# The output projection's and the MLP's lo parts on GpSimd: one operation of 1024 columns, or two of 512

## The chip, the cores and the metric

The kernel runs on one core of one Trainium2 chip. The metric is the device time of one execution in microseconds, the median over several runs. The engines are named as the profile names them: PE is TensorE (PEld its weight loads), DVE is VectorE, ACT is ScalarE, POOL is GpSimd, and SPq is the queue of SyncE, from which this kernel issues all of its DMAs.

## The reference, cut to what matters

Two layers of an encoder on a sequence of 1024 tokens, model width 1024, all in float32:

```python
h = rms_norm(x) * (1.0 + sc1) + sh1
z = h @ w_in[l]                       # three groups of heads: attention A, attention B, recurrence C
x = x + g1 * (jnp.concatenate([o_a, o_b, o_c], axis=-1) @ w_out[l])
h = rms_norm(x) * (1.0 + sc2) + sh2
x = x + g2 * (jnp.square(jax.nn.relu(h @ w_ff1[l])) @ w_ff2[l])     # 1024 -> 4096 -> 1024
```

## The kernel before, in words

Every product is made of three matmuls (`mm3`, lines 291 to 294): an operand is split into a rounded high part `hi` and a remainder `lo`, and hi by hi, hi by lo and lo by hi are added up in PSUM.

The weights come in **units** of 128 partitions by 1024 columns (`wunit`, lines 279 to 289). For each unit the SP queue issues one DMA of 512 KB into `w_raw` (line 284), ACT casts it into `w_hi` (line 286), and one subtraction makes `w_lo` (line 288). While the input projection runs, the subtraction is on DVE; from the end of the recurrence C on (`early_weights`), for the output projection and the whole MLP of that layer, it is on POOL: 224 of the 272 units.

From there on two pools are in use in turn (`wp = [f_["w"], w_first]`, rotated by `wunit`), each with one buffer for `w_raw` and two each for `w_hi` and `w_lo`. So a unit's DMA has to wait until the unit before it in the same pool has its `w_lo` (its raw buffer is free then), and a unit's cast has to wait until PE is done with the unit two places before it in the same pool.

The tokens are worked on in two halves of 512. The first half's output projection and a part of its MLP run while the second half's attention is still at work; then comes the second half's output projection, then groups of MLP weights used for both halves (`ffn_both`), and then the **last loop** of a layer: `ffn_half` of the second half alone over 8 groups. In `ffn_half` a group has four units: **a** and **b**, the two units of `w_ff1`, and **c** and **d**, the two units of `w_ff2`. They alternate between the pools: a and c are in one, b and d in the other. The code asks for the next group's a and b ahead of this group's c and d, so the order in one pool is c of the group before, next a, c, the a after it, and so on. PE uses each of these units for 24 matmuls with 512 columns. A product with a and b goes into a PSUM tile `mm`, then relu (ACT, 1119), square (ACT, 1120, and DVE, 1121) and a difference (POOL, 1122) make `act`; a product with c and d goes into PSUM tiles `S`, which DVE adds to x (1144).

The order of the instructions on each engine and in each queue isn't that of the text: the program is built with a scheduler that has a timing model of its own (`schedule_with_timeline_sim=True`) and puts each instruction where that model finds room. What stands in a queue is then worked off in that order.

Of the kernel before, what the change touches and what calls it, by code (L numbers as in the profile page):

```python
# [10 lines left out]
F32 = mybir.dt.float32  # L11
# [9 lines left out]
D = 1024  # L21
# [136 lines left out]
def tile_hybrid_encoder(ctx: ExitStack, tc: tile.TileContext, I, out, depth=DEPTH, dbg=None):  # L158
# [5 lines left out]
    def hp(k):  # L164
        return tc.high_priority(offset=HP[k]) if k in HP else nullcontext()
# [71 lines left out]
    def modulation_sums():  # L237

        while mod_pending:
            l, pc_, acc = mod_pending.pop(0)  # L240
            with hp("mod"):
                ps = (mmt, auxt)[MODAUX]()
                for j in range(4):
                    nc.tensor.matmul(ps[:, j:j + 1], acc[:, j * P:(j + 1) * P], ones[:, 0:1], start=True, stop=True)
            m = modc[l][:, pc_ * 4:pc_ * 4 + 4]
            nc.vector.tensor_add(m, m, ps[:, 0:4])
            if pc_ // 2 in (1, 4):
                nc.vector.tensor_scalar_add(m, m, 1.0)
# [26 lines left out]

    raw_bufs = [2]
    lo_eng = [nc.vector]

    def wunit(pool, src):
        if isinstance(pool, list):  # L280
            pool.append(pool.pop(0))
            pool = pool[-1]
        raw = pool.tile([P, D], F32, name="w_raw", tag="w_raw", bufs=raw_bufs[0])
        dma(raw, src)
        hi = pool.tile([P, D], F32R, name="w_hi", tag="w_hi")
        nc.scalar.copy(hi, raw)  # L286
        lo = pool.tile([P, D], F32R, name="w_lo", tag="w_lo")
        lo_eng[0].tensor_sub(lo, raw, hi.bitcast(F32))  # L288
        return hi, lo

    def mm3(ps, wh, wl, ah, al, first, last):
# [567 lines left out]
    def open_pools(specs):  # L859
        c = ExitStack()  # L860
        return c, {n: c.enter_context(tc.tile_pool(name=nm, bufs=b, side=sd)) for n, nm, b, sd in specs}
# [18 lines left out]
    def hook(j):  # L880
        if j == WAT:
            ready.extend(wunit(first_in[1]["w"], I["w_feat"][0, t]) for t in (T_BK, T_BQ))

    with hp("start"):
# [9 lines left out]
        for j in modulation_start(0, q0["m"], hook):  # L894
            b, c = modc[0][:, j:j + 1], modc[0][:, 8 + j:9 + j]
# [7 lines left out]
    for l in range(depth):  # L903
# [8 lines left out]
        wp, tp = w_["w"], w_["tp"]  # L912
        raw_bufs[0] = RAWA
        lo_eng[0] = nc.vector
        pp = const

        pc = pp.tile([P, 4], F32, name=f"pc{l}")
# [49 lines left out]
        def feat_tiles_(jobs):  # L967
            ws = [ready.pop(0) if ready else wunit(wp, I["w_feat"][l, j[0]]) for j in jobs]
            for half in range(2):
                for w, j in zip(ws, jobs):  # L970
                    ps = proj_feat(hT[half], w)
                    with hp('post'):
                        j[1](ps, half)

        def tok_group_(g, post):
            units = [wunit(wp, I["w_tok"][l, g, i]) for i in range(2)]
            for tt in range(0, NCH, 2):
                ps = proj_tok(hT, units, tt)
                with hp('post'):
                    post(ps, tt)  # L980
# [60 lines left out]
        def attend(tok):  # L1041
            k, pr, hq = tok[0], int(tok[1]), int(tok[2])
            with hp("att"):
                if k == "A":
                    attention_a(ap, l, (2 * pr, 2 * pr + 1), hq)
                else:
                    ap["ag"] = None
                    attention_b(ap, l, lamc, subg, (2 * pr, 2 * pr + 1), hq)

        def load_o(half, pool, rows, oT=None):  # L1050
            if oT is None:
                oT = [pool.tile([P, KT, HALF], F32R, name="oT", tag="h") for _ in range(2)]
            for j in rows:
                for i in range(2):
                    dma(oT[i].bitcast(F32)[:, j, :], s.o[j][i, :, half * HALF:(half + 1) * HALF])
            return oT

        for tok in ORDER.split():
            if tok == "C":
                modulation_sums()  # L1060
                wctx.close()
                hctx.close()
                octx, o_ = open_pools([("h", f"o{l}", 2, A)])
                heads0 = load_o(0, o_["h"], OPRE)
                bctx, b_ = open_pools([("c", f"cb{l}", 2, B)])
                cctx, c_ = open_pools([("c", f"ca{l}", 2, A)])

                def early_weights():
                    cctx.close()
                    raw_bufs[0] = 1  # L1070
                    lo_eng[0] = nc.gpsimd
                    wctx, w_ = open_pools([("w", f"w0_{l}", WFB // 2, A)])
                    return wctx, w_["w"], [wunit(w_["w"], I["w_out"][l, j]) for j in range(NEARLY)]

                early = []
                with hp("C"):
                    scan_c(c_["c"], b_["c"], l, pc[:, 3:4], lambda: early.append(early_weights()))
                bctx.close()
            elif tok[0] in "AB":
                attend(tok)  # L1080
            else:
                jobs[tok]()
# [207 lines left out]
```

## Time and profile before

| what | before |
|---|---|
| median of 3 runs | 3304.26 us (3304.03 to 3312.45) |
| the profiled execution, its own time | 3303.55 us |
| its span, first to last instruction | 3301.8 us |
| outside the span | 1.75 us |
| PE busy | 3150.7 us, 95% |
| mean granted clock of PE | 0.971 |
| POOL busy | 1304.7 us, 40%, of which 545.2 us is line 288 |

The time is the profiled execution's; the span is what its trace covers. Busy times of PE are modelled at their ends, so that a stretch in which PE waits for nothing shows 100%.

### The profile page before, as it was taken

How to read it: one execution, taken by the hardware profiler on the slowest of the kernel's cores; microseconds unless marked ns; L12 is line 12 of the kernel's file. 1: busy time of each engine (PE TensorE's matmuls, PEld its weight loads, DVE VectorE, ACT ScalarE, POOL GpSimd, SP SyncE). 2: the span in 40 equal slices, each digit the busy share in tenths (PEclk: the TensorE clock that was granted, in tenths of full speed). 3: DMA queues.
4: the chain of work that ended last, by engine and by line, in shares of the span. 5: the costliest groups of instructions: out<-in, count | busy, mean ns of one | idle time of the engine just before them, and what ended most of it. 6: DMA issues, size and time to landing. Idle time of an engine off the chain costs nothing.

```text
span 3301.8 us, 44789 instructions
## 1 busy us (share of the span) xinstructions
PE 3150.7 (95%) x16604; PEld 2541.8 (77%) x16604; DVE 1949.1 (59%) x2649; ACT 1478.6 (45%) x2847; POOL 1304.7 (40%) x867
## 2 busy tenths in 40 slices
PE   8999989999899999999999999899999999999998
PEld 4887767777678888887878966777777778888786
DVE  6577865557764565546463776555668545333545
ACT  4356656566652311213333666555677422222332
POOL 3343412334455433324534543123345443333453
PEclk8999979999999999999999999899999999999999
DMA  6665374435324244413234633734343421111222
GB/s 246 192 200 189 118 215 135 123 86 168 108 90 169 77 137 134 135 59 102 96 113 127 199 125 124 215 101 141 105 146 94 160 96 52 51 52 51 84 95 77
DMA packets 214458, 411.80 MB, mean 125 GB/s; under 512 B 35928, under 2 KB 92376, under 8 KB 213216
## 3 DMA queue, kind: packets, MB, share of 16 engines
q1 hardware_dynamic: 214240, 408.93, 39.2%
q8 instruction: 132, 2.16, 0.3%
q14 instruction: 86, 0.70, 0.1%
HBM read 335.43 MB, written 73.40 MB: 124 GB/s over the span
## 4 chain that ended last, share of the span: by engine, by line
PE 58%; DVE 6%; DMA 3%; ACT 2%; issue 2%; POOL 2%; SPq 0%; DVEq 0%; ACTq 0%; POOLq 0%
PE mm L292 10%; PE mm L293 10%; PE mm L294 10%; PE S L292 5%; PE S L293 5%; PE S L294 5%; PE aux L482 3%; PE S L450 2%; PE aux L474 2%; PE mm L780 1%; PE mm L403 1%; PE mm L745 1%; PE mm L402 1%; PE mm L404 1%; DVE col L456 1%
## 5 line engine op out<-in xcount | busy, mean ns | idle before, releaser
L288 POOL TENSOR_TENSOR w_lo<-w_raw,w_hi 128x1024 fp32r<-128x1024 f32 x224 | 545.2, 2443 | 490.6 <-ACT w_hi L286 475.3
L292 PE MATMUL mm<-h_hi,w_hi 128*128 128x512 f32 x1472 | 591.1, 403 | 7.9 <-ACT z L436 4.5
L293 PE MATMUL mm<-h_lo,w_hi 128*128 128x512 f32 x1472 | 584.1, 397 | 5.0 <-POOL h_lo L900 3.1
L294 PE MATMUL mm<-h_hi,w_lo 128*128 128x512 f32 x1472 | 580.4, 395 | 0.1
L286 ACT CAST w_hi<-w_raw 128x1024 fp32r<-128x1024 f32 x272 | 281.5, 1049 | 609.0 <-PE S L293 234.2
L456 DVE TENSOR_REDUCE col<-S 128x1 f32<-128x1024 f32 x288 | 350.1, 1224 | 116.9 <-PE S L450 115.6
L1144 DVE SCALAR_TENSOR_TENSOR x<-S,modc,x 128x512 f32<-128x512 f32 (+1 forms) x416 | 283.4, 724 | 228.3 <-PE S L294 228.1
L1121 DVE TENSOR_TENSOR ff_r<-ff_r 128x512 f32<-128x512 f32 x128 | 190.5, 1490 | 318.3 <-ACT act L1120 318.2
L458 ACT ACTIVATE pr<-S,col 128x1024 f32<-128x1024 f32 x288 | 323.8, 1125 | 120.9 <-DVE col L456 60.7
L292 PEld LDWEIGHTS mm<-h_hi,w_hi 128*128 128x128 f32 x1472 | 279.5, 190 | 78.5 <-ACT z L436 5.8
L293 PEld LDWEIGHTS mm<-h_lo,w_hi 128*128 128x128 f32 x1472 | 279.9, 190 | 73.1 <-POOL h_lo L900 5.1
L294 PEld LDWEIGHTS mm<-h_hi,w_lo 128*128 128x128 f32 x1472 | 279.9, 190 | 63.5 <-DVE w_lo L288 0.8
L1122 POOL TENSOR_TENSOR act<-ff_r,act 128x512 fp32r<-128x512 f32 x128 | 169.2, 1322 | 397.6 <-DVE ff_r L1121 394.5
L292 PE MATMUL S<-act,w_hi 128*128 128x512 f32 (+1 forms) x832 | 318.7, 384 | 3.4 <-DVE x L1144 3.2
L293 PE MATMUL S<-act,w_hi 128*128 128x512 f32 (+1 forms) x832 | 317.5, 382 | 1.5 <-POOL act L1122 1.5
L294 PE MATMUL S<-act,w_lo 128*128 128x512 f32 (+1 forms) x832 | 315.0, 382 | 0.8 <-POOL w_lo L288 0.8
L450 PE MATMUL S<-ks,qs 128*128 128x512 f32 x768 | 247.7, 430 | 36.2 <-ACT pr L458 18.9
L1119 ACT ACTIVATE ff_r<-mm 128x512 f32<-128x512 f32 x128 | 76.2, 595 | 409.6 <-PE mm L294 405.6
L474 PE MATMUL aux<-cst,pr 128*128 128x128 f32 x1536 | 234.2, 287 | 19.4 <-DVE pr L590 8.5
L474 PEld LDWEIGHTS aux<-cst,pr 128*128 128x128 f32 x1536 | 188.4, 147 | 67.3 <-issue 18.2
L482 PE MATMUL aux<-pt,vt 128*64 128x256 f32 x1536 | 195.8, 387 | 3.7 <-ACT pt L475 3.7
L475 ACT COPY pt<-aux 128x512 f32<-128x512 f32 x288 | 166.3, 592 | 69.7 <-PE aux L474 68.5
(233 smaller groups left out, 5908.7 us busy)
## 6 DMA issues: line engine op xcount, KB each, us to landing
w_raw<-in_w_ff SPq DMA_DIRECT2D x192, 512.0 KB, 3.3
mw<-in_w_mod SPq DMA_DIRECT2D x160, 256.0 KB, 2.9
ks<-bk SPq DMA_DIRECT2D x192, 128.0 KB, 3.2
lf<-g_st SPq DMA_DIRECT2D x64, 256.0 KB, 3.2
oT<-o SPq DMA_DIRECT2D x64, 256.0 KB, 5.3
lf<-lf SPq DMA_DIRECT2D x16, 1024.0 KB, 5.1
w_raw<-in_w_out SPq DMA_DIRECT2D x32, 512.0 KB, 3.4
w_raw<-in_w_feat SPq DMA_DIRECT2D x28, 512.0 KB, 3.8
```

Source lines behind the costliest of these rows:

```text
L286: nc.scalar.copy(hi, raw)
L288: lo_eng[0].tensor_sub(lo, raw, hi.bitcast(F32))
L292: nc.tensor.matmul(ps, wh, ah, start=first, stop=False)
L293: nc.tensor.matmul(ps, wh, al, start=False, stop=False)
L294: nc.tensor.matmul(ps, wl, ah, start=False, stop=last)
L450: nc.tensor.matmul(sp[:, hh * HALF:(hh + 1) * HALF], q[:, sl], ks[:, hh * HALF:(hh + 1) * HALF], start=i == 0, stop=i == len(qs) - 1)
L456: nc.vector.tensor_reduce(nm, sp, axis=AX.X, op=ALU.max, negate=True)
L458: nc.scalar.activation(p, sp, AF.Exp, bias=nm, accum_out=z)
L474: nc.tensor.transpose(tp[:, j * P:(j + 1) * P], p[:, kt * P:(kt + 1) * P], ident)
L482: nc.tensor.matmul(ps[64 * c:64 * c + 64, 0:256], vt[:, kt, :], pts[c][kt // 4][:, kt % 4, :], start=kt == 0, stop=kt == KT - 1)
L1121: nc.vector.tensor_mul(r, r, r)
L1144: nc.vector.scalar_tensor_tensor(x, sp[:, k * HALF:k * HALF + n], g2[:, j - 1 + k:j + k], x, op0=ALU.mult, op1=ALU.add)
```

## The change

From `early_weights` on, POOL makes each `w_lo` in two subtractions of 512 columns. On DVE it stays one.

```diff
--- before.py
+++ after.py
@@ -275,6 +275,7 @@
     raw_bufs = [2]
     lo_eng = [nc.vector]
+    lo_parts = [1]
@@ -285,7 +286,9 @@
         lo = pool.tile([P, D], F32R, name="w_lo", tag="w_lo")
-        lo_eng[0].tensor_sub(lo, raw, hi.bitcast(F32))
+        n = D // lo_parts[0]
+        for c in range(0, D, n):
+            lo_eng[0].tensor_sub(lo[:, c:c + n], raw[:, c:c + n], hi.bitcast(F32)[:, c:c + n])
         return hi, lo
@@ -912,6 +915,7 @@
         lo_eng[0] = nc.vector
+        lo_parts[0] = 1
@@ -1069,6 +1073,7 @@
                     lo_eng[0] = nc.gpsimd
+                    lo_parts[0] = 2
```

The four new lines shift the numbers: `wunit`'s DMA, cast and difference are 284, 286 and 288 before and 285, 287 and 291 after; `mm3` is 292 to 294 before and 295 to 297 after; relu, square and difference of `act` are 1119, 1120 and 1122 before and 1124, 1125 and 1127 after.

The scheduler's order changes too, in four stretches: layer 0 and layer 1 where the first half's output projection runs beside attention (770 to 990 us and 2370 to 2530 us of the trace before), and the last loop of either layer (1483 to 1670 us and 3070 to 3270 us). Elsewhere, apart from a few single swaps, it is the same. The three places below are in the last loop of layer 0; the number in a name counts the tiles as the program makes them, so that c is 13487 (raw; 13489 hi, 13491 lo) before and 13575 (13577, 13579) after, the next a 13559 (13561) before and 13649 (13651, 13653) after, d 13493 before and 13582 after, b of the next group 13565 before and 13656 after.

The SP queue before, DMAs of the weights of the loop, from a of one group on:

```order
L284 DMA w_raw_13413<-in_w_ff1 128x1024
L284 DMA w_raw_13419<-in_w_ff1 128x1024
L284 DMA w_raw_13487<-in_w_ff2 128x1024
L284 DMA w_raw_13493<-in_w_ff2 128x1024
L284 DMA w_raw_13559<-in_w_ff1 128x1024
L284 DMA w_raw_13565<-in_w_ff1 128x1024
L284 DMA w_raw_13633<-in_w_ff2 128x1024
```

And after:

```order
L285 DMA w_raw_13499<-in_w_ff1 128x1024
L285 DMA w_raw_13432<-in_w_ff2 128x1024
L285 DMA w_raw_13575<-in_w_ff2 128x1024
L285 DMA w_raw_13506<-in_w_ff1 128x1024
L285 DMA w_raw_13582<-in_w_ff2 128x1024
L285 DMA w_raw_13649<-in_w_ff1 128x1024
L285 DMA w_raw_13725<-in_w_ff2 128x1024
L285 DMA w_raw_13656<-in_w_ff1 128x1024
```

Before, the units stand in the order a, b, c, d; after, the pool with a and c is one unit ahead of the other one (the c after next, 13725, stands ahead of b, 13656).

ACT before, in the same loop, from the cast of b of one group to that of b of the next; `ff_r` and `act` are relu and square:

```order
L286 CAST w_hi_13421<-w_raw_13419 128x1024
L1119 ACTIVATE ff_r_13336<-mm_13310 128x512
L1120 ACTIVATE act_13335<-ff_r_13336 128x512
L286 CAST w_hi_13489<-w_raw_13487 128x1024
L286 CAST w_hi_13495<-w_raw_13493 128x1024
L1119 ACTIVATE ff_r_13451<-mm_13425 128x512
L1120 ACTIVATE act_13450<-ff_r_13451 128x512
L286 CAST w_hi_13561<-w_raw_13559 128x1024
L1119 ACTIVATE ff_r_13482<-mm_13456 128x512
L1120 ACTIVATE act_13481<-ff_r_13482 128x512
L286 CAST w_hi_13567<-w_raw_13565 128x1024
```

And after:

```order
L287 CAST w_hi_13508<-w_raw_13506 128x1024
L287 CAST w_hi_13577<-w_raw_13575 128x1024
L1124 ACTIVATE ff_r_13539<-mm_13513 128x512
L287 CAST w_hi_13651<-w_raw_13649 128x1024
L1125 ACTIVATE act_13538<-ff_r_13539 128x512
L287 CAST w_hi_13584<-w_raw_13582 128x1024
L1124 ACTIVATE ff_r_13570<-mm_13544 128x512
L1125 ACTIVATE act_13569<-ff_r_13570 128x512
L287 CAST w_hi_13658<-w_raw_13656 128x1024
```

The cast of the next a (13651) stands ahead of that of d (13584) now.

PE before, where the next a (w_hi_13561) is used first; the rows ahead of it are the last of the first 24 matmuls with c and d (w_hi_13489, w_hi_13495):

```order
L292 MATMUL S_13514<-act_13304,w_hi_13489 128x512
L293 MATMUL S_13514<-act_13304,w_hi_13489 128x512
L294 MATMUL S_13514<-act_13304,w_lo_13491 128x512
L292 MATMUL S_13514<-act_13335,w_hi_13495 128x512
L293 MATMUL S_13514<-act_13335,w_hi_13495 128x512
L294 MATMUL S_13514<-act_13335,w_lo_13497 128x512
L292 MATMUL mm_13571<-h_hi_10421,w_hi_13561 128x512
L293 MATMUL mm_13571<-h_lo_10422,w_hi_13561 128x512
L292 MATMUL mm_13602<-h_hi_10421,w_hi_13567 128x512
L293 MATMUL mm_13602<-h_lo_10422,w_hi_13567 128x512
L294 MATMUL mm_13571<-h_hi_10421,w_lo_13563 128x512
```

And after, from the end of the matmuls with b of the group before (w_hi_13508) on:

```order
L295 MATMUL mm_13544<-h_hi_10465,w_hi_13508 128x512
L296 MATMUL mm_13544<-h_lo_10466,w_hi_13508 128x512
L297 MATMUL mm_13544<-h_hi_10465,w_lo_13510 128x512
L295 MATMUL S_13589<-act_13388,w_hi_13577 128x512
L296 MATMUL S_13589<-act_13388,w_hi_13577 128x512
L297 MATMUL S_13589<-act_13388,w_lo_13579 128x512
L295 MATMUL mm_13663<-h_hi_10465,w_hi_13651 128x512
L296 MATMUL mm_13663<-h_lo_10466,w_hi_13651 128x512
L295 MATMUL S_13604<-act_13388,w_hi_13577 128x512
L296 MATMUL S_13604<-act_13388,w_hi_13577 128x512
L297 MATMUL S_13604<-act_13388,w_lo_13579 128x512
L297 MATMUL mm_13663<-h_hi_10465,w_lo_13653 128x512
```

The first matmul with the next a has moved from behind 24 matmuls with c and d to behind the first three with c. Counted in the whole order of PE, from the start of the last matmul with the `w_hi` of the c before (13343 before, 13427 after) to the first with this next a stand 57 matmuls before and 25 after. The same holds, with 58 before and 25 after, for the next a of the four groups that follow; the groups ahead of these five in that loop and the last loop of layer 1 do not have it.

## Rows read from the trace of the kernel before

**Rows 1.** The page: busy time, share of the span and instructions of each engine, and the busy tenths of PE and its granted clock in 40 slices of the span.

```profile
PE 3150.7 (95%) x16604; PEld 2541.8 (77%) x16604; DVE 1949.1 (59%) x2649; ACT 1478.6 (45%) x2847; POOL 1304.7 (40%) x867
PE   8999989999899999999999999899999999999998
PEclk8999979999999999999999999899999999999999
```

**Rows 2.** Windows: a stretch, its length, the busy time of each engine in it, the granted clock of PE, the DMA share and GB/s. First output projection beside attention, layer 0 (two rows); MLP of layer 0 up to its last loop; the last loop of layer 0; first output projection beside attention, layer 1; MLP of layer 1; its last loop.

```profile
core 0: us, PE busy (x) PEld busy (x) DVE busy (x) ACT busy (x) POOL busy (x), PEclk, DMA share, GB/s
768.00:870.00 102.00, 90.99 (x468) 69.62 (x466) 72.32 (x89) 63.47 (x111) 46.13 (x28) 0.92 0.50 149
870.00:1000.00 130.00, 125.03 (x628) 97.10 (x627) 91.52 (x115) 78.19 (x136) 62.84 (x36) 0.97 0.30 93
1000.00:1480.00 480.00, 477.05 (x2119) 389.18 (x2118) 258.29 (x328) 112.21 (x149) 178.00 (x92) 1.00 0.37 117
1540.00:1670.00 130.00, 130.00 (x567) 106.05 (x566) 57.42 (x61) 38.58 (x48) 74.81 (x38) 1.00 0.29 94
2370.00:2530.00 160.00, 149.29 (x816) 113.84 (x815) 123.84 (x160) 112.10 (x201) 77.04 (x45) 0.98 0.43 131
2530.00:3070.00 540.00, 539.25 (x2413) 438.03 (x2412) 247.09 (x286) 153.38 (x223) 212.33 (x113) 1.00 0.23 76
3130.00:3270.00 140.00, 139.13 (x603) 112.69 (x602) 64.22 (x67) 40.44 (x50) 79.53 (x40) 1.00 0.29 94
```

**Rows 3.** The page's groups: line, engine, operation, out<-in with shapes, count | busy us, mean ns of one | idle time of the engine just before, and what ended most of it. POOL's two subtractions, DVE's square, and PE's matmuls with a `w_lo`.

```profile
L288 POOL TENSOR_TENSOR w_lo<-w_raw,w_hi 128x1024 fp32r<-128x1024 f32 x224 | 545.2, 2443 | 490.6 <-ACT w_hi L286 475.3
L294 PE MATMUL mm<-h_hi,w_lo 128*128 128x512 f32 x1472 | 580.4, 395 | 0.1
L1121 DVE TENSOR_TENSOR ff_r<-ff_r 128x512 f32<-128x512 f32 x128 | 190.5, 1490 | 318.3 <-ACT act L1120 318.2
L1122 POOL TENSOR_TENSOR act<-ff_r,act 128x512 fp32r<-128x512 f32 x128 | 169.2, 1322 | 397.6 <-DVE ff_r L1121 394.5
L294 PE MATMUL S<-act,w_lo 128*128 128x512 f32 (+1 forms) x832 | 315.0, 382 | 0.8 <-POOL w_lo L288 0.8
```

**Rows 4.** The timeline (start us, us, engine, line, operation) at one turn of the last loop of layer 0: the last matmul with the `w_hi` of the c before (PE, 1547.00), the casts of c and d (ACT), the subtraction of c (POOL), the DMA of the next a (SPq), its cast (ACT), its subtraction (POOL), and the first matmul with it (PE, 1560.13).

```profile
1547.00 0.39 PE L293 MATMUL S<-act,w_hi 128*128 128x512 f32 x1
...
1547.42 2.00 ACT L286 CAST w_hi<-w_raw 128x1024 fp32r<-128x1024 f32 x2 [11.47 <-PE S L293]
...
1548.61 2.41 POOL L288 TENSOR_TENSOR w_lo<-w_raw,w_hi 128x1024 fp32r<-128x1024 f32 x1 [4.62 <-ACT w_hi L286]
...
1551.04 0.33 SPq L284 DMA_DIRECT2D w_raw<-in_w_ff  x1
...
1554.27 1.05 ACT L286 CAST w_hi<-w_raw 128x1024 fp32r<-128x1024 f32 x1 [3.68 <-DMA w_raw<-in_w_ff]
...
1555.45 2.41 POOL L288 TENSOR_TENSOR w_lo<-w_raw,w_hi 128x1024 fp32r<-128x1024 f32 x1 [0.36 <-ACT w_hi L286]
...
1560.13 0.40 PE L292 MATMUL mm<-h_hi,w_hi 128*128 128x512 f32 x1
```

**Rows 5.** Waits of the SP queue, the longest of all: who waited for whom, us in total, times, longest.

```profile
SPq L284 <- POOL w_lo L288: 1162.5, 204, 34.9
```

**Rows 6.** Windows of one group each in the last loop of layer 0, the first and the last of five (columns as in rows 2).

```profile
1554.70:1576.80 22.10, 22.10 (x98) 18.02 (x97) 10.00 (x10) 6.67 (x9) 12.14 (x7) 1.00 0.31 100
...
1643.10:1665.20 22.10, 22.10 (x98) 18.03 (x97) 9.58 (x10) 6.38 (x9) 12.15 (x7) 1.00 0.29 95
```

**Rows 7.** Windows with PE alone: a stretch in which PE did almost nothing and the stretch behind it, three times (length, PE busy, granted clock, DMA share, GB/s).

```profile
1688.70:1691.80 3.10, 0.00 (x0) 1.00 0.85 244
1692.10:1698.90 6.80, 6.13 (x14) 0.50 0.27 85
...
2472.30:2474.90 2.60, 0.02 (x1) 1.00 0.81 214
2474.90:2481.70 6.80, 6.08 (x40) 1.00 0.33 109
1533.20:1534.70 1.50, 0.00 (x0) 1.00 0.00 0
1534.70:1541.50 6.80, 6.79 (x30) 1.00 0.22 77
```

**Rows 8.** The timeline of DVE and POOL at three places: DVE's square (1121) with POOL idle, then behind POOL's operations, then a DVE operation on one column behind POOL's 288 beside attention.

```profile
1194.52 0.69 DVE L1121 TENSOR_TENSOR ff_r<-ff_r 128x512 f32<-128x512 f32 x1
...
1301.85 2.40 POOL L288 TENSOR_TENSOR w_lo<-w_raw,w_hi 128x1024 fp32r<-128x1024 f32 x1 [3.08 <-ACT w_hi L286]
...
1302.35 2.45 DVE L1121 TENSOR_TENSOR ff_r<-ff_r 128x512 f32<-128x512 f32 x1 [8.41 <-ACT act L1120]
...
1304.88 1.29 POOL L1122 TENSOR_TENSOR act<-ff_r,act 128x512 fp32r<-128x512 f32 x1 [0.63 <-DVE ff_r L1121]
...
858.65 2.35 POOL L288 TENSOR_TENSOR w_lo<-w_raw,w_hi 128x1024 fp32r<-128x1024 f32 x1 [3.93 <-ACT w_hi L286]
...
858.88 2.14 DVE L585 SCALAR_TENSOR_TENSOR col<-rr,lam,col 128x1 f32<-128x1 f32 x1
```

## The prediction

> **What bounds the kernel now.** Three views, in this order. The page's first part and its strips: PE is busy 95% of the span, and its granted clock is at or near full speed except at the start, beside attention and at the end [rows 1]. So only three things can change the time: work on PE (none is added or taken away here), stretches in which PE waits, and stretches in which its clock is granted at 0.50. Second, the windows by stage [rows 2]. In the MLP stretches PE is busy for nearly all of the time at a clock of 1.00 (477.05 of 480 us, 130.00 of 130, 539.25 of 540, 139.13 of 140): nothing there can be gained, and anything that makes PE wait is lost in full. Beside attention PE is free for 11.0, 5.0 and 10.7 us, 26.7 in all; only there is something to gain. Third, the groups [rows 3]: before PE's matmuls with a `w_lo` of POOL stands idle time of 0.1 us (tiles `mm`) and 0.8 us (tiles `S`, all of it ended by POOL). The wait that a sooner first half of `w_lo` could shorten is under 1 us in 3302.
>
> **The change part by part.** *POOL's own time.* One subtraction of 1024 columns takes 2.40 to 2.41 us when undisturbed [rows 4, 8]; the nearest row for one of 512 columns is POOL's subtraction for `act`, same types, 1.29 us [rows 8]. Two of them are 2.58, some 0.17 more; for 224 units that is 38 us on an engine that is busy for 40% of the span, with 490.6 us of idle time just ahead of these very operations [rows 1, 3]. As PE waits for them under 1 us, its direct cost is 0 to 1 us; I take 0. If the cover were gone, it would be at most 38 us. In return the first half of a `w_lo` is there 1.1 us sooner, which is worth the 0.9 us above at most.
>
> *The order.* What moves is more than the cost of the operation, since the scheduler built another order on it. One turn of layer 0's last loop shows what a next a needs [rows 4]: the last matmul with the `w_hi` of the c before starts at 1547.00; its buffer free, ACT casts c at 1547.42; POOL subtracts from 1548.61; the DMA of the next a is issued at 1551.04, just as that subtraction ends, because this pool has one raw buffer (the queue's longest wait of all is of this kind, 1162.5 us in 204 times [rows 5]); the cast starts when the data is there, at 1554.27, and takes 1.05. So the next a can be used from 1555.32, 8.32 us after 1547.00. PE first wants it at 1560.13: 4.8 us to spare.
>
> Now the distance in PE's order. In this loop a group is 96 matmuls (four units of 24), and takes 22.10 us [rows 6]: 0.230 us each. Before, 57 matmuls lie between the two points: 13.1 us, as the timeline shows (1560.13 less 1547.00). After, it is 25: 5.75 us. The chain of cast, subtraction, DMA and cast doesn't get shorter: it gets the 0.17 of the split longer, since the raw buffer is free only after the second half. So PE, which takes its instructions in order, comes to the next a at 5.75 and can go on at 8.32 + 0.17 + some 0.1 for the signal = 8.59: it waits 2.8 us. Behind it stand the remaining matmuls with c and d, ready but queued. Five matmuls later (1.15 us) it wants the first half of that unit's `w_lo`, which is there 0.13 + 1.29 + 0.1 = 1.5 us after the cast, with 0.1 of it gone when PE starts: 0.25 us more. That is 3.05 per group. It isn't won back later, as the next turn of the chain starts from PE's last matmul with c, which has moved back by as much. The order has this in five groups: **5 x 3.05 = 15.3 us**. From below: if the signals cost nothing and the half comes in time, 5 x 2.7 = 13.5; from above, POOL busy with the unit of the other pool when c's or a's subtraction is due, one operation of 1.29 more in each group: 22.
>
> *PE's clock.* After 3.10 us in which PE did nothing it was granted 0.50 for the next 6.8 us, with 14 matmuls where some 30 are usual; after 2.60 and after 1.50 us of nothing it stayed at 1.00 [rows 7]. A wait of 2.8 lies between. A stretch of 6.8 us at half speed costs 3.4 us. Bounds: 0 to 5 x 3.4 = 17 us; I take half of it, **8.5 us**, since 2.8 is no nearer to the one row than to the other.
>
> *Beside attention.* In the two stretches where the scheduler mixed softmax and projection anew, the work is the same and PE has 26.7 us free of which some may go or as much may come; nothing in the orders says which. DVE is helped there a little by the split (rival F). I take **-2 us**, within 10 either way. In layer 1's last loop the new order leaves 37 matmuls between the two points once, and 51 or more in the other groups; 8.59 us are 37 matmuls: 0.
>
> Sum: 15.3 + 8.5 - 2 = 21.8 on the profiled execution's own 3303.55 (span 3301.8 and 1.75 around it): 3325.4. The median of the runs shown is 0.7 above that execution: **3326 us**.
>
> **The rivals.** *F, faster.* The square on DVE reads two operands from SBUF; it takes 0.69 us with POOL idle, 2.45 when it starts 0.5 us after a subtraction of POOL: it ends 0.55 after POOL's 2.40 [rows 8], and its mean is 1490 ns [rows 3]. Beside attention a DVE operation on a single column took 2.14 us for the same reason [rows 8]. With halves DVE waits for 1.29 at most, not 2.40. In the MLP no one on PE's side waits for DVE, so it is worth nothing there; beside attention it could at most halve PE's 26.7 free us: 13 us, 3291. It decides the outcome only if it is worth over 15, that is if the five waits don't come at all. The Trainium skill, "SBUF — State Buffer", section "SBUF: two separate sides", states that DVE with two SBUF inputs and GpSimd lock each other out of a shared pair of ports for the whole of an instruction; the trace agrees (0.69 alone, 2.45 behind), and by that rule alone halves would make the kernel faster, 3291 against the 3326 of the sum. 0.08.
>
> *S, same.* The waits come, but without a fall of the clock, and the stretches beside attention give back more than 5.5 us: 15.3 - 6 and less, 3313 and below. Or the change of order is covered because the next a's DMA lands sooner than 3.2 us. Speaking for it: PE's free time there is large enough. Against: nothing points to a gain of that size, and the chain of rows 4 is tight, one link after another. 0.18.
>
> *H, all five clocks.* Every wait is followed by a stretch at 0.50: 15.3 + 17 - 2, 3334 us; with the orders beside attention worse by 10, 3344. 0.24.
>
> *Forecast.* The five waits with none to four falls of the clock: 3314 to 3334. 0.50.
>
> **How the numbers follow.** About 0.3%, 10 us, is what a measurement of this kernel can tell from no change. Slower by more than that (above 3314): the forecast and H, 0.74. Within: 0.18. Faster: 0.08. The range of 8 in 10 leaves out F and the upper end of H, and takes in most of S: 3307 to 3341.
>
> **What would show it.** In the profile after: POOL 448 operations of some 1.29 us; in layer 0's last loop five gaps of PE of 2.6 to 3.2 us, each ended by ACT's cast of a `w_hi` (line 287), five groups of some 25 us in place of 22.10, with or without a granted clock of 0.50 behind them; the other MLP stretches as before; DVE's square with a mean well below 1490 ns. I'm wrong if PE has no waits for a cast in that loop (the chain was shorter or the order not as read), if gaps beside attention shrink or grow by more than 10 us, or if the waits come with a different length: the term at risk most is the clock, for which no row has 2.8 us.

## The result: faster, and the profile after

The changed kernel takes 3286.58 us in the median of 4 runs (3284.74 to 3288.06), before 3305.01 in the median of 4: 0.9935 of before, 95% interval 0.9923 to 0.9948. That is 18 us or 0.65% less, where the sum gave 21.8 more. The profiled execution took 3288.06 us with a span of 3285.8, so 16.0 less span than before. The page after, its first part and the strips that answer to [rows 1]:

```profile
PE 3144.1 (96%) x16604; PEld 2539.3 (77%) x16604; DVE 1850.1 (56%) x2649; ACT 1479.4 (45%) x2847; POOL 1374.1 (42%) x1091
PE   7998989999999999999999989899999999999998
PEclk8999989999999999999999999899999999999999
```

The groups that answer to [rows 3] (columns as there):

```profile
L291 POOL TENSOR_TENSOR w_lo<-w_raw,w_hi 128x512 fp32r<-128x512 f32 x448 | 616.5, 1402 | 459.1 <-ACT w_hi L287 449.2
L297 PE MATMUL mm<-h_hi,w_lo 128*128 128x512 f32 x1472 | 582.7, 396 | 0.2
L1126 DVE TENSOR_TENSOR ff_r<-ff_r 128x512 f32<-128x512 f32 x128 | 132.0, 1033 | 349.0 <-ACT act L1125 339.4
L1127 POOL TENSOR_TENSOR act<-ff_r,act 128x512 fp32r<-128x512 f32 x128 | 172.8, 1352 | 349.3 <-DVE ff_r L1126 346.8
L297 PE MATMUL S<-act,w_lo 128*128 128x512 f32 (+1 forms) x832 | 316.1, 382 | 0.0
```

POOL has 69 us more to do and PE doesn't wait for it (0.8 us ahead of the matmuls with `S` before, 0.0 now). DVE has 99 us less, 58.5 of them in its square, which takes 1033 ns in the mean, not 1490.

Where the 16 us went is told by PE's own work. In most places the same set of matmuls lies behind PE in both programs, so the time at which the next one starts can be compared. The table gives the change of that difference over a stretch (bounds in the time of before, us; negative is faster). It is worked out from the starts in the traces, also for the runs of the next section; "old" marks a stretch in which the program has the order and the one subtraction of before.

| kernel | 765 to 926, layer 0 beside attention | 926 to 1543, MLP | 1543 to 1700, last loop | 2365 to 2540, layer 1 beside attention | 3098 to 3200, its last loop |
|---|---|---|---|---|---|
| changed | -11.0 | -4.7 | 0.0 | +2.0 | -2.2 |
| changed, again | -10.0 | -4.3 | +1.0 | -4.7 | -2.2 |
| halves, old order | -2.5 | -4.1 | +0.5 | +4.1 | -0.9 |
| whole, new order | -7.2 | -1.3 | +2.0 | -0.8 | -2.2 |
| quarters, new order | -7.8 | -3.8 | -0.5 | -2.2 | -2.2 |
| layer 0 alone | -9.9 | -4.8 | +0.9 | +4.2 (old) | +0.3 (old) |
| layer 1 alone | +3.8 (old) | -0.3 (old) | -0.7 (old) | -3.1 | -2.2 |
| c waits for c | -11.4 | -4.3 | +30.9 | -3.9 | -2.2 |

The cells marked old (up to 4.2 us) and the stretches that the change doesn't touch (0 to 765 and 1700 to 2365 us, from -5.2 to +5.6) show what one trace differs from another by itself. In the MLP of layer 1, 2540 to 3098 us, it is less: all traces lie within -1.4 to +1.5 there. Beyond that stand 10 to 11 us in layer 0 beside attention, 4 to 5 in the MLP behind it and 2.2 in layer 1's last loop, the same in every trace with its new order. In the last loop of layer 0, where 15.3 us of waits and half of the clock's 17 were forecast, stands nothing at all.

The first stretch in windows (columns as in [rows 2]); of before:

```profile
764.90:925.60 160.70, 144.38 (x724) 109.82 (x724) 122.64 (x152) 102.76 (x182) 72.93 (x43) 0.93 0.43 128
```

Of after, that stretch and two groups of the last loop of layer 0:

```profile
766.20:915.90 149.70, 138.18 (x724) 104.85 (x723) 117.86 (x151) 100.60 (x178) 78.52 (x56) 0.98 0.45 137
...
1541.00:1563.10 22.10, 22.10 (x98) 18.01 (x97) 8.40 (x10) 6.34 (x9) 13.54 (x11) 1.00 0.28 96
1629.40:1651.50 22.10, 22.10 (x97) 18.02 (x96) 8.49 (x10) 6.34 (x9) 13.65 (x11) 1.00 0.30 96
```

Beside attention PE's free time fell from 16.3 to 11.5 us, and its busy time for the same 724 matmuls from 144.4 to 138.2, as the granted clock rose from 0.93 to 0.98. So more than half of these 11 us came from the clock. The groups of the last loop take 22.10 us, to the hundredth what they took before [rows 6].

PE's two longest gaps in that stretch of before end at 774.10 (3.15 us) and at 860.23 (3.58). Behind the first the granted clock was 0.50. What the new order did to the second is seen in the SP queue (start, us, queue or engine, line, operation; `ks` and `qs` are attention's keys and queries). Before, under the window behind the first gap (columns as in [rows 7]):

```profile
774.10:780.80 6.70, 6.58 (x27) 0.50 0.75 187
...
852.99 0.32 SPq L498 DMA_DIRECT2D o<-o_hi  x1
853.41 0.38 SPq L284 DMA_DIRECT2D w_raw<-in_w_ff  x1
853.88 0.41 SPq L567 DMA_DIRECT2D ks<-bk  x1
...
855.13 1.38 SPq L567 DMA_DIRECT2D ks<-bk  x3
...
860.23 1.19 PE L450 MATMUL S<-ks,qs 128*128 128x512 f32 x2 [3.58 <-DMA qs<-bq]
```

And after, the same loads of keys and the same matmul:

```profile
850.64 1.71 SPq L570 DMA_DIRECT2D ks<-bk  x4
...
853.84 0.37 SPq L501 DMA_DIRECT2D o<-o_hi  x1
...
855.29 0.50 PE L453 MATMUL S<-ks,qs 128*128 128x512 f32 x1 [0.29 <-ACT pr L461]
...
855.57 0.43 SPq L285 DMA_DIRECT2D w_raw<-in_w_ff  x1
```

Before, the four loads of keys for this matmul stand in the queue behind a store of attention's output, which goes out at 852.99, when ACT has made it, and behind a unit of weights; now they stand ahead of both. The last matmul with the keys that held their buffer starts at 852.34 before and at 850.21 after; the issue of the four loads is done 4.2 us later before and 2.1 us later after. (The profile names the load of `qs` that follows; by the built program the late operands are these keys.) In the three traces with layer 0 in the old order, runs 2 and 6 among them, this matmul waits 2.53 to 3.58 us; in the six with the changed kernel's order there, run 3 with its whole subtractions among them, 0.30 at most. So this wait went with the order, not with the halves. The gap at 774.10 goes the same way: 2.89 to 3.15 us in the old order, 1.17 to 2.01 in the new one.

Why no wait came in the last loop of layer 0 is seen in the timeline of after, at the turn that the prediction had worked out (start, us, engine, line, operation):

```profile
1528.78 0.40 PE L296 MATMUL mm<-h_lo,w_hi 128*128 128x512 f32 x1
...
1529.21 1.05 ACT L287 CAST w_hi<-w_raw 128x1024 fp32r<-128x1024 f32 x1 [2.01 <-PE mm L296]
...
1530.39 2.53 POOL L291 TENSOR_TENSOR w_lo<-w_raw,w_hi 128x512 fp32r<-128x512 f32 x2 [0.52 <-ACT w_hi L287]
...
1532.95 0.33 SPq L285 DMA_DIRECT2D w_raw<-in_w_ff  x1
...
1535.19 0.39 PE L296 MATMUL S<-act,w_hi 128*128 128x512 f32 x1
...
1536.23 1.05 ACT L287 CAST w_hi<-w_raw 128x1024 fp32r<-128x1024 f32 x1 [5.48 <-DMA w_raw<-in_w_ff]
...
1540.98 0.40 PE L295 MATMUL mm<-h_hi,w_hi 128*128 128x512 f32 x1
```

The cast at 1529.21 is that of c (13575). It doesn't wait for the last matmul with the c before, which starts at 1535.19. It follows the one at 1528.78, which is the last with the a in between. In the built program c has the `w_hi` buffer of that a now, and the next a that of the c before; before the change c took the buffer of the c before. So the chain of cast, subtraction, DMA and cast begins 6.4 us sooner than the prediction let it begin, the next a is ready at 1537.28 (1536.23 and 1.05), and PE comes to it at 1540.98 with 3.7 us to spare. It is the next a that needs the last matmul with the c before now; that one starts at 1535.19, and the cast of the next a starts only at 1536.23, when its data is there.

### The profile page after: what moved, and what is told of

Read it like the earlier page. It is cut to its first block, busy times and chain, and to the rows that moved or that the text cites. A ratio compares the mean times of both kernels' runs of the same rounds, so it can differ in the third digit from the quotient of the medians.

```text
span 3285.8 us, 45091 instructions
## 1 busy us (share of the span) xinstructions
PE 3144.1 (96%) x16604; PEld 2539.3 (77%) x16604; DVE 1850.1 (56%) x2649; ACT 1479.4 (45%) x2847; POOL 1374.1 (42%) x1091
## 4 chain that ended last, share of the span: by engine, by line
PE 77%; DVE 8%; DMA 6%; ACT 3%; issue 2%; POOL 2%; SPq 1%; DVEq 0%; ACTq 0%; POOLq 0%
PE mm L295 12%; PE mm L296 12%; PE mm L297 12%; PE S L295 5%; PE S L296 5%; PE S L297 5%; PE aux L485 4%; PE S L453 4%; PE aux L477 4%; PE mm L783 3%; PE mm L748 1%; PE mm L405 1%; PE mm L406 1%; PE mm L407 1%; DMA mw<-in_w_mod 1%
## 5 line engine op out<-in xcount | busy, mean ns | idle before, releaser
L291 POOL TENSOR_TENSOR w_lo<-w_raw,w_hi 128x512 fp32r<-128x512 f32 x448 | 616.5, 1402 | 459.1 <-ACT w_hi L287 449.2
L461 ACT ACTIVATE pr<-S,col 128x1024 f32<-128x1024 f32 x288 | 323.7, 1124 | 125.6 <-DVE col L459 65.2
L1126 DVE TENSOR_TENSOR ff_r<-ff_r 128x512 f32<-128x512 f32 x128 | 132.0, 1033 | 349.0 <-ACT act L1125 339.4
L477 PEld LDWEIGHTS aux<-cst,pr 128*128 128x128 f32 x1536 | 188.2, 147 | 64.1 <-issue 13.4
```

What stands on the lines that cost most here:

```text
L291: lo_eng[0].tensor_sub(lo[:, c:c + n], raw[:, c:c + n], hi.bitcast(F32)[:, c:c + n])
L461: nc.scalar.activation(p, sp, AF.Exp, bias=nm, accum_out=z)
L477: nc.tensor.transpose(tp[:, j * P:(j + 1) * P], p[:, kt * P:(kt + 1) * P], ident)
```

## The experiments

Four questions: is it the shorter subtraction or the new order (2, 3, 4), which layer (5, 6), is a better order the rule (7), and was the buffer the only wrong link in the chain (8). Runs 2, 3, 4 and 8 keep the scheduler's order: they exchange instructions at their place after the scheduler has put the program in order. (`_narrow(i, c, n)` is instruction i on n columns from column c.) All ratios are to the kernel before on the same chip, where its median was 3308.7 to 3309.5 us.

**1. The changed kernel again.**

> The changed kernel once more, on the chip of the next three, as their yardstick: 3285 to 3288 us, ratio to before 0.993 to 0.995.

Measured 3284.03 us, 0.9926 (0.9912 to 0.9939), just outside the time and the ratio expected. The gain stands, on this chip 25 us.

**2. Halves in the old order.**

```diff
 (kernel before; after scheduling, for each subtraction of w_lo on POOL)
+        first = _narrow(i, 0, D // 2, name=..., sync_info=mybir.SyncInfo(on_wait=s.on_wait, on_update=[]))
+        second = _narrow(i, D // 2, D // 2, sync_info=mybir.SyncInfo(on_wait=[], on_update=s.on_update))
+        b.instructions[k:k + 1] = [first, second]
```

> The kernel before with its order kept instruction by instruction on every engine; only each 1024-column subtraction on POOL is replaced, at its place, by two of 512, the first with its waits, the second with its signal. Theory H (the halves themselves: DVE gets in between two of them and is not held up for a whole 2.4 us): all or nearly all of the 18 us come, 3286 to 3290 us, and DVE's square has a mean near 1030 ns. Theory O (the new order beside attention made the gain; halves are worth only the waits of PE for DVE and POOL in the MLP, 2.1 + 1.5 + 0.9 + 0.8 us in the trace of before): 3298 to 3303 us, though the square's mean falls just the same. In between, both hold a share.

Measured 3301.61 us, 0.9973 (0.9961 to 0.9984). The time is inside the range of O, but before took 4 us more on this chip than in the result; by the ratio it is some 9 us, between the theories and nearer to O. The square fell to 993 ns in the mean, as both said. The window of the first stretch shows that the clock gained little here and PE's free time hardly changed (16.1 us against 16.3):

```profile
764.70:922.80 158.10, 142.01 (x724) 107.35 (x723) 118.06 (x151) 101.89 (x179) 76.25 (x56) 0.95 0.44 132
```

In the MLP it has nearly the whole gain of the changed kernel (-4.1 of -4.7). What it took away there is seen in PE's waits (who waited for whom: us, times, longest) from 926 to 1543 us, of before:

```profile
PE S L292 <- DVE x L1144: 2.3, 4, 1.6
PE S L293 <- POOL act L1122: 1.5, 1, 1.5
```

and at the same work with halves in the old order:

```profile
PE S L292 <- DVE x L1144: 1.8, 2, 1.1
```

The wait for `act`, 1.5 us, is gone. How it came about shows in rows of before:

```profile
1518.45 2.90 DVE L348 SCALAR_TENSOR_TENSOR x<-x,modc,n_y 128x512 f32<-128x512 f32 x1
...
1532.19 0.68 DVE L1121 TENSOR_TENSOR ff_r<-ff_r 128x512 f32<-128x512 f32 x1
...
1534.71 0.50 PE L293 MATMUL S<-act,w_hi 128*128 128x512 f32 x1 [1.52 <-POOL act L1122]
```

The square itself takes 0.68 us there. It is late because three operations ahead of it in DVE's queue, the one at 1518.45 the first, took 2.89 to 2.90 us behind subtractions of POOL, where others of their kind took 0.74. With halves the ones held up at this place take 1.72 to 1.78. The waits shown make up 2.0 of the 4.1 us; where the rest comes from they don't show.

**3. Whole subtractions in the new order.**

```diff
 (changed kernel; after scheduling, for each pair)
+        if i.outs[0].offset == 0:
+            b.instructions[k] = _narrow(i, 0, D - 8)
+        else:
+            b.instructions[k] = _narrow(i, D - 8, 8)
```

> The changed kernel with its order kept on every engine; the first of each pair of subtractions on POOL is widened to 1016 columns and the second narrowed to the last 8, so that POOL holds DVE up for about 2.4 us again. Theory H: the gain is gone, 3302 to 3310 us, square near 1490 ns. Theory O: it stays but for the MLP's waits, 3287 to 3293 us. In both, POOL gets some 0.2 us slower a unit for the small second operation, which is covered.

Measured 3298.06 us, 0.9966 (0.9955 to 0.9978): some 11 us from the order alone. In the MLP little of the gain is left (-1.3). But the stretch begins with the end of attention, where PE waits 1.4 us for softmax's `pr` in this trace and not in that of before; and the 1.5 us wait for `act` at its end is gone here too, as in every program whose layer 0 has halves or the new order. Beside layer 0's attention most of the gain is there, with the clock of after:

```profile
769.10:922.70 153.60, 139.28 (x725) 105.41 (x723) 122.11 (x149) 100.39 (x176) 78.39 (x57) 0.98 0.45 135
```

So both theories hold a share. The two ratios multiplied give 0.9939; the changed kernel has 0.9926 with an interval that reaches to it. Within what these runs can tell, halves and order add up.

**4. Quarters in the new order.**

```diff
 (changed kernel; after scheduling, for each half)
+        first = _narrow(i, lo, D // 4, name=..., sync_info=mybir.SyncInfo(on_wait=s.on_wait, on_update=[]))
+        second = _narrow(i, lo + D // 4, D // 4, sync_info=mybir.SyncInfo(on_wait=[], on_update=s.on_update))
```

> The changed kernel with its order kept; each half is split in place into two subtractions of 256 columns. Theory H: DVE is held up for 0.75 us at most in place of 1.3, so a part of the gain comes once more, 3278 to 3284 us, square near 850 ns. Theory O: no more to gain, 3285 to 3289 us. POOL takes some 0.35 us more a unit (estimate: twice the 0.17 that two halves take more than one whole), which lengthens the chain to the next DMA of a pool by as much.

Measured 3286.65 us, 0.9939 (0.9927 to 0.9951): no further gain. The square's durations (ns: least, median, most; first and last start) show how long DVE was held up. In the old order, before and with halves (run 2):

```profile
L1121 DVE TENSOR_TENSOR ff_r<-ff_r x128: 673/1735/2919, 903.2 to 3262.4; 128x512 f32<-128x512 f32 x128
L1121 DVE TENSOR_TENSOR ff_r<-ff_r x128: 674/715/2541, 900.4 to 3255.8; 128x512 f32<-128x512 f32 x128
```

In the new order, whole (run 3), in halves (after) and in quarters:

```profile
L1126 DVE TENSOR_TENSOR ff_r<-ff_r x128: 674/1463/2690, 898.5 to 3252.3; 128x512 f32<-128x512 f32 x128
L1126 DVE TENSOR_TENSOR ff_r<-ff_r x128: 675/868/2876, 889.9 to 3246.7; 128x512 f32<-128x512 f32 x128
L1126 DVE TENSOR_TENSOR ff_r<-ff_r x128: 672/806/1932, 893.9 to 3245.4; 128x512 f32<-128x512 f32 x128
```

The first cut takes 1020 ns off the median in the old order and 595 in the new one, the second 62, and already with halves PE waits only 0.3 us for DVE in the MLP of layer 0. POOL pays 83 us more of its own (1374.1 to 1457.5), hidden again.

**5 and 6. One layer alone.**

```diff
-                    lo_parts[0] = 2
+                    lo_parts[0] = 2 if l == 0 else 1     # 6: l == 1
```

> Two halves in layer 0 alone; layer 1 has one subtraction of 1024, in the order of the kernel before. Theory A (the gain sits beside layer 0's attention, where the trace of after is 11.0 us ahead of before, and PE's clock is granted at 0.98 where it was 0.93): most of the gain, 0.994 to 0.996 of before, some 3288 to 3292 us on a chip where before takes 3305. Theory B (halves help alike everywhere): half of the gain, 0.9965, some 3296.

> Two halves in layer 1 alone, layer 0 in the order of the kernel before with one subtraction of 1024. Theory A: within 0.25% of before, 0.9975 to 1.0005 (the 2.2 us of its last loop are sure, beside its attention the traces of one and the same program differ by 6.7 us). Theory B: half of the gain, 0.9965.

Measured 3291.32 us, 0.9944 (0.993 to 0.9958), with layer 0 alone, and 3299.57 us, 0.9973 (0.996 to 0.9987), with layer 1 alone. Three quarters of the gain lie in layer 0, as theory A says, and run 5's interval leaves out theory B (0.9965). Run 6 is just outside A's range, and its interval holds both theories. Its trace shows 2.2 us in the last loop and 1.1 in the MLP ahead of it; the rest is inside what two traces of one program differ by beside attention. In layer 0 this kernel has the instructions of the kernel before, and its window repeats the clock (0.93), with 19.3 us free:

```profile
769.70:934.20 164.50, 145.21 (x724) 110.78 (x724) 123.24 (x152) 103.02 (x182) 72.88 (x43) 0.93 0.42 125
```

**7. Quarters with the scheduler's own order.**

```diff
-                    lo_parts[0] = 2
+                    lo_parts[0] = 4
```

> Four subtractions of 256 columns in the source, so that the scheduler makes an order of its own for them. If shorter subtractions lead the scheduler to a better order beside attention as a rule, 0.992 to 0.995 of before, as with two. If the order of after is a lucky one, this one lies anywhere from 0.994 to 1.002: the halves alone are worth 0.997 by the run in the old order, and its own order may add or take.

Measured 3296.09 us, 0.9958 (0.9944 to 0.9973). The same quarters in the order of the changed kernel had 0.9939 (run 4): by these ratios the scheduler's own order for quarters is worth some 6 us less, but the intervals overlap. The ratio lies outside what a better order as a rule would give, 0.992 to 0.995, though its interval reaches into it, and inside what a lucky one would: nothing here says that a shorter subtraction leads the scheduler to the better order by itself.

**8. The buffer that the prediction had assumed.**

```diff
 (changed kernel; after scheduling, for the pairs of c and next a in layer 0's last loop)
+        late = [w for w in casts["w_hi_%d" % a][2].sync_info.on_wait if w.ant_name.startswith("PE")]
+        rest = [w for w in s.on_wait if not w.ant_name.startswith("PE")]
+        b.instructions[k] = i.__replace__(sync_info=mybir.SyncInfo(on_wait=rest + late, on_update=s.on_update))
+        if n % 2 == 0:
+            x, y = where["w_hi_%d" % c], where["w_hi_%d" % a]
+            x.addr, y.addr = y.addr, x.addr
```

> The changed kernel, same order on every engine, but in layer 0's last loop the unit c gets the w_hi buffer that the prediction gave it, that of the c before, and the next a that of the a before it; so the cast of c waits for PE's last matmul with the c before, about 1535.2 in the trace of after, where it now waits for the last with a, 1528.8. If the step that failed is this one (which buffer c takes) and the rest of the chain was right, PE waits five times for the cast of a next a, 2.7 to 3.1 us each, 13.5 to 15.3 in all and 22 at most, with half-clock stretches of 3.4 us behind none to five of them: 0.3 to 0.9 % slower than the changed kernel, 0.996 to 1.003 of before. If something else in the chain was wrong as well (the DMA lands sooner, the cast is quicker), no wait appears and it is the changed kernel's time, 0.992 to 0.995 of before.

Measured 3316.17 us, 1.0021 (1.0008 to 1.0034): by the two ratios 0.96% slower than the changed kernel (run 1), and slower than before. All of it is in this loop (+30.9 in the table). Its timeline at the same turn:

```profile
1530.23 1.05 ACT L287 CAST w_hi<-w_raw 128x1024 fp32r<-128x1024 f32 x1 [8.57 <-PE S L296]
...
1531.41 2.55 POOL L291 TENSOR_TENSOR w_lo<-w_raw,w_hi 128x512 fp32r<-128x512 f32 x2 [7.08 <-ACT w_hi L287]
...
1533.99 0.33 SPq L285 DMA_DIRECT2D w_raw<-in_w_ff  x1
...
1537.31 1.04 ACT L287 CAST w_hi<-w_raw 128x1024 fp32r<-128x1024 f32 x1 [5.54 <-DMA w_raw<-in_w_ff]
...
1538.40 0.80 PE L295 MATMUL mm<-h_hi,w_hi 128*128 128x512 f32 x1 [2.71 <-ACT w_hi L287]
```

PE's waits in this kernel from 1530 to 1690 us:

```profile
PE mm L295 <- ACT w_hi L287: 13.4, 5, 2.8
PE S L295 <- ACT w_hi L287: 3.5, 1, 3.5
PE S L297 <- POOL w_lo L291: 2.0, 1, 2.0
PE mm L297 <- POOL w_lo L291: 0.6, 1, 0.6
```

and a group, then the ten us behind the first wait and behind the last of the five, as windows:

```profile
1538.40:1565.40 27.00, 24.23 (x97) 19.13 (x97) 7.78 (x10) 6.26 (x9) 13.50 (x11) 0.94 0.25 79
...
1538.40:1548.40 10.00, 9.99 (x37) 8.11 (x38) 4.08 (x5) 2.54 (x4) 8.42 (x6) 0.83 0.34 107
...
1645.50:1655.50 10.00, 10.00 (x42) 7.67 (x43) 5.00 (x6) 2.76 (x5) 8.44 (x6) 1.00 0.33 107
```

Five waits of 2.60 to 2.76 us for the cast of a next a, a link-by-link copy of the chain in [rows 4], where 2.8 was worked out. A group takes 26.6 to 27.0 us in place of 22.10 where the clock falls. So in this chain the buffer was the link that failed, and the only one. Behind four of the five waits the clock was lower, 0.83 over ten us, which costs 1.7 (10 x 0.17). The five groups cost 13.4 + 0.6 + 4 x 1.7 = 20.8; the last 10 of the 30.9 us stand at the end of the loop, where PE waits another 3.5 and 2.0 us for the cast and the subtraction of the last d and the clock falls once more (0.66 over ten us, 3.4).

## Why the prediction was wrong, point by point

**The step that failed** is in the part on the order: "the last matmul with the `w_hi` of the c before starts at 1547.00; its buffer free, ACT casts c". That was a reading of the trace of before, and true there. The prediction then counted, in the new order, the matmuls between that point and the next a, 25, and took for granted that c would wait for the same point, PE's last use of the unit two places before it in the pool. But that is the turn in the order of before, and two buffers are not a fixed turn. With the new order c took the buffer that was free sooner, that of the a, and its cast started at 1529.21, not after 1535.19. The count of 25 was right and was counted from the wrong matmul. So both terms that stand on this wait, 15.3 us and 8.5 for the clock, measured 0.0. Which instruction the cast of c waits for could have been read from the built program beforehand, like the order itself.

By the traces the sum missed by 37.8 us (21.8 more forecast, 16.0 less measured): 23.8 in this loop, 7.0 beside attention (-9.0 in the two layers together, -2 forecast), 4.7 in the MLP of layer 0 and 2.2 in layer 1's last loop, where nothing was forecast.

**The size of what would have followed** was near by run 8: 2.8 a wait against 2.60 to 2.76, five of them, and 21 us for the five groups against 23.8 of waits and clock. The waits fit (13.4 against 5 x 2.8), while the 5 x 0.25 for the first half of `w_lo` came to one wait of 0.6, for another unit. That the clock fits is in part luck: a fall costs 1.7 us and not 3.4, but four of five waits had one, where half was taken. The 6.8 us at 0.50 in [rows 7] are a stretch behind a gap at another place, and were not a price for every gap.

**POOL's time** was sized at 1.29 us an operation and 38 us in all. Its median is 1295 ns, as the durations of line 291 after show (ns: least, median, most; first and last start):

```profile
L291 POOL TENSOR_TENSOR w_lo<-w_raw,w_hi x448: 1258/1295/2282, 753.8 to 3250.6; 128x512 fp32r<-128x512 f32 x150
```

But the mean is 1402, as some last far longer: 71 us for the line. They are the ones held up by DVE in their turn. In this trace a DVE operation on two SBUF operands was still running, for 0.2 us or more, at the start of 105 of the 448; 104 of these took over 1.5 us, and none of the other 343 did. It cost nothing, as foreseen.

**Beside attention** -2 us within 10 either way was taken; it was -10 to -11 in layer 0. The sum there counted the 26.7 us in which PE does nothing and left out that PE's busy time holds stretches at half clock, in those same rows of [rows 2] (0.92 and 0.97). With shorter gaps both came back: 4.8 us of idle time and 6.2 of clock. That "nothing in the orders says which" doesn't hold for one gap at least: in the SP queue the loads that PE waited for moved ahead of a store and a unit of weights. (The low tenths of the clock strip in [rows 1] are in its first, sixth and 26th slices and not, as the prediction reads it, beside attention and at the end; nothing hangs on it, as [rows 2] have the clock there.)

**Rival F** (0.08) is what happened in sign and in time, 3291 against 3287, but not by its reason alone, and the time was luck: its 13 us were half of PE's free time beside attention, and what came was order, clock and MLP as well. Halves by themselves, with which DVE gets in between, are worth 0.27% by run 2, and in that run's trace 4 us are in the MLP, where the prediction said that no one on PE's side waits for DVE and that nothing can be gained. By [rows 2] 2.95 us are left there, and the 1.50 us of nothing at 1533.20 in [rows 7] are the wait for `act`. The other share, 0.34% by run 3, came from the order, of which F said nothing; which of the two is larger the intervals don't tell.

**What stays open.** Of the moved instructions beside attention one group, the loads of keys at 850.64, is read from a wait above; no run moved it alone, and which of the others shorten PE's gaps there is not known. That the clock rose because these gaps became shorter is argued from the rows and was not tried by itself. That layer 1 alone gives 0.27% is measured; its trace places 3 us of these 9.

## What to carry to other kernels

Where a new order shortens a distance, first find out what the late instruction waits for in the new program; a wait read from the trace of before belongs to the buffers of before. Price a stretch beside softmax by its idle time and by its clock together: here, as two gaps of 3 us became shorter, both came back. Look in the DMA queue for loads that stand behind a transfer which itself waits. A long subtraction on GpSimd with its operands in SBUF is cheaply cut in two where VectorE stands behind it; a second cut gave nothing here.

## What the runs showed of the hardware that was not expected

A waiting DVE operation gets in between two subtractions of POOL that stand back to back: halving them cut the square's median from 1735 to 715 ns with the same order of instructions on every engine (run 2, in run 4's rows). One such turn in run 2's trace:

```profile
1498.34 1.30 POOL L288 TENSOR_TENSOR w_lo<-w_raw,w_hi 128x512 fp32r<-128x512 f32 x1 [5.92 <-ACT w_hi L286]
...
1498.77 1.41 DVE L329 TENSOR_TENSOR n_acc<-n_acc,n_sq 128x512 f32<-128x512 f32 x1 [0.78 <-ACT n_sq L325]
...
1499.59 1.74 POOL L288 TENSOR_TENSOR w_lo<-w_raw,w_hi 128x512 fp32r<-128x512 f32 x1
```

DVE's operation, 0.69 us when it has no POOL operation beside it, ends 0.54 us after the first half; the second half lasts until 1501.33, 1.74 us and not 1.30. So POOL pays 0.44 us for letting DVE in. The clock behind a gap is no fixed price: 0.83 over ten us behind the gap of 2.71 us that ended at 1538.40, 1.00 behind the one of 2.60 that ended at 1645.49, in one trace and the same loop; two traces of one and the same program differ by 6.7 us beside layer 1's attention (changed, +2.0 and -4.7).
